# Norm of the output blocks in four parts, feed-forward h rows on GpSimd's queue, and first h rows of the last embedding block ahead of its weights

## The chip, the cores and the metric

The kernel runs on one core of a Trainium2 chip. A core has a matrix engine (TensorE, PE in the profile, with PEld for its weight loads), a vector engine (VectorE, DVE), a scalar engine (ScalarE, ACT), GpSimd (POOL) and a sync engine (SyncE, SP) that here only issues transfers. Each of them works through its own queue of instructions in order. Transfers between the chip's memory (HBM, tensors named `_d` here) and the core's working memory (SBUF) are issued from SP, ACT and POOL. The matrix engine writes its sums into eight accumulator banks (PSUM).

The metric is the device time of one execution in microseconds (us). Before the change it is 2998.36 us, the median of three runs from 2993.83 to 3000.24.

## The reference, cut to what matters

One layer of a hybrid decoder on 2048 prompt tokens and 32 sample tokens, 2080 rows in all, with a model width of 1024, all in float32. Everything up to `mix` (projections, recurrence, attention) is the first part of the kernel and is not touched. What the change touches is the second part:

```python
mix = concat(o_a, o_b)                       # (tokens, 1024)
h = x + mix @ w_o

hn = rmsnorm(h, norm_ffn_g)
u = hn @ w_gate                              # D_FF = 2816
c = conv_b + sum(conv_w[j] * shifted(u, j) for j in range(3))
h = h + (silu(c) * (hn @ w_up)) @ w_down

gate = sigmoid(rmsnorm(h, norm_ple_g) @ w_ple_gate)
h = h + gate * (p_emb @ w_ple_proj)          # PLE_DIM = 256
y = rmsnorm(h, norm_final_g)
```

`rmsnorm(x, g)` is `x * rsqrt(mean(x * x) + 1e-6) * g` along the width of 1024.

## The kernel before

**Tiling.** The second part is the function `trunk`. Activations lie transposed: a tile has 128 features as partitions and tokens along it, so that the width of 1024 makes `NK` = 8 tiles, called rows here (row m of h is `h[m]`, 128 features by a block's tokens). The tokens make three blocks of 696, 696 and 688 (`TRUNK`, L38). Every float32 product is made of three matmuls of rounded halves (`mm3`, L144): high by high, high by low and low by high. So weights and activations are split into a high and a low half, by a cast on ACT and a subtraction on DVE (`split_to`, L183 to L186; `halves`, L1085).

**Stages.** Nine blocks run one after the other (L1559 to L1565): output blocks 0, 1, 2 (`out_block`, the product with w_o), feed-forward blocks 0, 1, 2 (`ffn_block`), embedding blocks 0, 1, 2 (`embed_block`). Each has a generator (`out_prep`, `ffn_prep`, `embed_prep`) that loads and splits its input rows; the block before runs it ahead in steps (`ahead`, `s.to`). Between the stages the rows go through HBM: `h_d` (h after w_o), `hn_d` (its norm times the gain), `h2_d` (h after the feed-forward part). The profile leaves a trailing digit out of a name, so both `h_d` and `h2_d` stand in it as `h_d`; the line tells them apart (L1431 loads h_d, L1314 stores and L1447 and L1483 load h2_d).

**Output block.** It multiplies by w_o row by row, adds x, stores the row to h_d (L1128) and sums squares. The norm comes in two delayed steps in the queue `late` (L1091, L1172): `cols` makes the reciprocal root of each token's mean square; `norm` (L1159) spreads it over the partitions by matmuls against the identity and then, for each of the eight rows, multiplies by it and by the gain on DVE (L1162) and stores the row to hn_d (L1163). `flush(n)` runs up to n entries of `late`. Blocks 0 and 1 are flushed in the next output block (L1115 the first entry, L1140 after m == 2 the rest); block 2 is flushed in feed-forward block 0, at f == 2, one entry after product 5 and one after product 4 of the gate (L1349). Block 2's rows lie in the pool of eight `held` tiles (L1122), and a held tile is free again when its last user, for norms the store to hn_d, is done.

**Feed-forward block.** It goes over 22 tiles of the width of 2816 in pairs (f = 0, 2, ... 20). A pair's product with w_gate, and then with w_up, is a 2 by 2 block product in seven instead of eight products (`strassen`, L1243), made in the order `USE` = 1, 5, 6, 7, 4, 2, 3. After products 1, 6 and 7 the accumulator is copied out on ACT (`copied`, L1254, tile `s`); DVE adds combine banks (L1265, L1269, L1271). `after_gate(n)` and `after_up(n)` are called after product n and put in between what else is due: pieces of the down product (`down`) and `flush`. In block 0 the weight combinations are made on GpSimd (`factors`, L168) and stored; in blocks 1 and 2 they are loaded.

**Down product.** Two pairs at a time (the eleventh alone) are multiplied with w_down, again in seven products in the order `DOWN_USE` = 1, 6, 7, 4, 5, 3, 2 (`downs`, L1286). Their weights are fetched from `wd_d` on GpSimd's queue (L1296, 512 KB each, into six tiles), two products ahead. DVE adds each sum into a row of h (L1312). `ADD` (L1284) says into which half: products 1, 6, 3 and 2 go to rows 0 to 3, products 7, 4 and 5 to rows 4 to 7. The h rows are loaded from h_d at the end of f == 2, into held tiles (L1428 to L1431), and after the last group each finished row is stored to h2_d (L1313, L1314). The last group of a block is left to the start of the next block (L1325) or, in block 2, done at its end (L1435).

**Embedding block.** `embed_prep` loads the h2 rows, scales and splits them, and then loads and splits the two rows of pT. `embed_block` makes the first two (block 2: three) rows of the product with w_ple_gate for all k at once (`dense_first`, L1475), runs one entry of `late`, and asks for the first two h2 rows again (`more`, L1485 and L1486) for the addition at L1502. Each later `embed` asks for one more. The tiles come from `wide`, 44 of 128 by 696, which most of the trunk shares; raw weights from a pool of seven, split ones from a pool of six.

**What sets the order.** The program is written in the order above, but a planner sets each engine's queue from the program's order (earlier is more urgent), the dependencies, the free tiles and its own estimate of times (`schedule_with_timeline_sim`, L1687). A transfer written late can be put early if its tile is free. Once the queues are set, each engine waits at its next instruction.

## Time and profile before

| | before |
|---|---|
| median of 3 runs | 2998.36 us (2993.83 to 3000.24) |
| profiled execution | 2996.88 us |
| its span, first to last instruction | 2995.1 us |
| mean granted clock of the matrix engine | 0.987 |
| PE busy from 1850 to 2000 us | 146.88 of 150 us |
| PE busy from 2000 to 2200 us | 200.00 of 200 us |
| PE busy from 2900 to 2950 us | 46.27 of 50 us |
| h rows loaded from h_d (L1431) | 24, first and last issue at 1436.9 and 2315.4 us |
| rows stored to h2_d (L1314) | 24, from 1837.2 to 2740.4 us |
| rows loaded again from h2_d (L1483) | 24, from 2746.4 to 2939.0 us |
| down weights from wd_d (L1296) | 231 |

The profile's times are in us from the start of the span. A page gives the busy time of each engine; the 40 slices give the busy share in tenths; the view of waits sums up who waited for whom ("PE mm L146 <- ACT s L1254" is PE, about to run a matmul of line 146 into tile mm, held up by the instruction of line 1254 on ACT); the timeline lists instructions with start, length and, in brackets, the idle time before them and what ended it. SPq stands for SP's queue of transfers. "x3" behind a row means three merged ones, whose length runs from the first to the last.

The time up to about 1215 us belongs to the first part. Output blocks run to about 1390 us, feed-forward block 0 to about 1830, block 1 to about 2270, block 2 to about 2740, and the embedding blocks to the end.

### The profile page before, as it was taken

How to read it: one execution, taken by the hardware profiler on the slowest of the kernel's cores; microseconds unless marked ns; L12 is line 12 of the kernel's file. 1: busy time of each engine (PE TensorE's matmuls, PEld its weight loads, DVE VectorE, ACT ScalarE, POOL GpSimd, SP SyncE). 2: the span in 40 equal slices, each digit the busy share in tenths (PEclk: the TensorE clock that was granted, in tenths of full speed). 3: DMA queues.
4: the chain of work that ended last, by engine and by line, in shares of the span. 5: the costliest groups of instructions: out<-in, count | busy, mean ns of one | idle time of the engine just before them, and what ended most of it. 6: DMA issues, size and time to landing. Idle time of an engine off the chain costs nothing.

```text
span 2995.1 us, 52434 instructions
## 1 busy us (share of the span) xinstructions
PE 2899.1 (97%) x18895; PEld 2700.5 (90%) x18895; DVE 2163.4 (72%) x4717; ACT 1318.4 (44%) x2856; POOL 674.0 (23%) x792
## 2 busy tenths in 40 slices
PE   8999999999989898999999999999999999999998
PEld 8987789887777677999999999999999999999998
DVE  6656758657386467569987888766679777677777
ACT  5333423222276576335444444544444544444443
POOL 1443222212143563103443431000001000000000
PEclk9999999999999999999999999999999999999998
DMA  5898634324349996766766668777779777778773
GB/s 179 297 355 305 206 105 120 99 80 124 123 114 279 249 234 177 258 233 210 243 203 204 203 200 293 236 242 243 252 242 308 251 237 243 245 261 295 267 268 132
DMA packets 342036, 659.88 MB, mean 220 GB/s; under 512 B 62928, under 2 KB 134736, under 8 KB 339984
## 3 DMA queue, kind: packets, MB, share of 16 engines
q1 hardware_dynamic: 304928, 468.42, 49.0%
q0 software_dynamic: 33264, 121.13, 12.8%
q10 hardware_dynamic: 3584, 66.98, 6.2%
q8 instruction: 149, 2.44, 0.3%
q14 instruction: 111, 0.91, 0.1%
HBM read 509.46 MB, written 213.92 MB: 242 GB/s over the span
## 4 chain that ended last, share of the span: by engine, by line
PE 59%; issue 17%; DMA 10%; DVE 9%; POOL 2%; ACT 2%; SPq 1%; POOLq 0%; DVEq 0%; ACTq 0%
PE mm L146 13%; PE mm L148 13%; PE mm L147 13%; PE mm L348 2%; PE mm L349 2%; PE mm L350 2%; POOL w L1296 1%; DMA cf<-coef_d 1%; PE acc L839 1%; PE PT L827 1%; PE S L814 1%; DMA xr<-in_xT_dram 1%; PE lv L485 1%; DVE w L185 1%; DMA draw<-in_w_down_dram 1%
## 5 line engine op out<-in xcount | busy, mean ns | idle before, releaser
L147 PE MATMUL mm<-w 128*128 128x348 f32 (+3 forms) x3636 | 1166.1, 321 | 1.3 <-DVE w L1456 0.8
L146 PE MATMUL mm<-w 128*128 128x348 f32 (+3 forms) x3508 | 1108.7, 323 | 18.7 <-ACT s L1254 6.2
L148 PE MATMUL mm<-w 128*128 128x348 f32 (+3 forms) x3508 | 1117.3, 321 | 2.0 <-DVE w L185 2.0
L147 PEld LDWEIGHTS mm<-w 128*128 128x128 f32 x3636 | 684.1, 188 | 4.1 <-DVE w L1088 2.0
L146 PEld LDWEIGHTS mm<-w 128*128 128x128 f32 x3508 | 656.2, 188 | 26.6 <-ACT s L1254 8.7
L148 PEld LDWEIGHTS mm<-w 128*128 128x128 f32 x3508 | 659.0, 188 | 3.3 <-DVE w L185 2.6
L185 DVE TENSOR_TENSOR w<-raw,w 128x512 fp32r<-128x512 f32 x586 | 421.1, 723 | 176.2 <-ACT w L184 168.6
L184 ACT CAST w<-raw 128x512 fp32r<-128x512 f32 x586 | 360.9, 621 | 413.1 <-PE mm L148 288.8
L1296 POOL DMA_DIRECT2D w<-wd_d x231 | 124.3, 538 | 899.2 <-PE mm L148 793.4
L1312 DVE TENSOR_TENSOR h<-h,mm 128x348 f32<-128x348 f32 (+1 forms) x504 | 247.7, 507 | 44.8 <-PE mm L148 43.5
L820 ACT ACTIVATE P<-P,st 128x256 f32<-128x256 f32 (+3 forms) x256 | 134.0, 526 | 60.0 <-DVE st L819 56.4
L1254 ACT COPY s<-mm 128x348 f32<-128x348 f32 (+1 forms) x198 | 88.0, 445 | 152.2 <-PE mm L148 151.9
L819 DVE CUSTOM_DVE_ANT_0 P<-S,mask 128x256 f32<-128x256 f32 (+3 forms) x256 | 104.4, 448 | 62.0 <-PE S L815 40.2
L348 PE MATMUL mm<-wh,xh 128*128 128x512 f32 x352 | 140.8, 403 | 0.1
L349 PE MATMUL mm<-wl,xh 128*128 128x512 f32 x352 | 140.7, 401 | 0.2 <-DVE wl L271 0.2
L350 PE MATMUL mm<-wh,xl 128*128 128x512 f32 x352 | 140.3, 399 | 0.0
L146 PE MATMUL mm<-xh,wh 128*128 128x384 f32 (+2 forms) x384 | 124.6, 329 | 8.0 <-ACT xh L246 5.2
L148 PE MATMUL mm<-xh,wl 128*128 128x384 f32 (+2 forms) x384 | 124.4, 328 | 4.2 <-DVE wl L271 4.2
L147 PE MATMUL mm<-xl,wh 128*128 128x384 f32 (+2 forms) x384 | 125.0, 328 | 1.2 <-DVE xl L247 1.2
L185 DVE TENSOR_TENSOR dw<-draw,dw 128x512 fp32r<-128x512 f32 x77 | 75.3, 981 | 54.0 <-ACT dw L184 53.6
L152 POOL TENSOR_SCALAR wh<-wraw 128x512 fp32r<-128x512 f32 x96 | 75.3, 798 | 133.3 <-PE mm L147 41.6
L814 PE MATMUL S<-kH,qS 128*128 128x256 f32 (+3 forms) x256 | 98.6, 400 | 6.7 <-DVE st L819 4.2
(346 smaller groups left out, 5053.2 us busy)
## 6 DMA issues: line engine op xcount, KB each, us to landing
w<-wd_d POOLq DMA_DIRECT2D x231, 512.0 KB, 5.5
wd_d<-dw SPq DMA_DIRECT2D x77, 512.0 KB
out_sk_dram<-in_cache_k_dram ACTq DMA_DIRECT2D x56, 584.0 KB
out_sv_dram<-in_cache_v_dram ACTq DMA_DIRECT2D x56, 584.0 KB
raw<-in_w_gate_dram SPq DMA_DIRECT2D x110, 256.0 KB
raw<-in_w_up_dram SPq DMA_DIRECT2D x110, 256.0 KB
wraw<-in_w_in_dram SPq DMA_DIRECT2D x104, 256.0 KB
raw<-w_gate_d SPq DMA_DIRECT2D x88, 256.0 KB
```

The source lines that it names most:

```text
L146: PE.matmul(ps, lhsT=wh, rhs=xh, start=first, stop=False, skip_group_check=read)
L147: PE.matmul(ps, lhsT=wh, rhs=xl, start=False, stop=False, skip_group_check=read)
L148: PE.matmul(ps, lhsT=wl, rhs=xh, start=False, stop=last, skip_group_check=read)
L184: A.copy(w[:, 0], raw)
L185: V.tensor_sub(w[:, 1], raw, f32(w[:, 0]))
L348: PE.matmul(ps, lhsT=xh[k][:, js], rhs=wh, start=k == 0, stop=False)
L349: PE.matmul(ps, lhsT=xh[k][:, js], rhs=wl, start=False, stop=False)
L350: PE.matmul(ps, lhsT=xl[k][:, js], rhs=wh, start=False, stop=k == NK - 1)
L814: PE.matmul(s[:, w * i:w * i + w], lhsT=bl.q(hh), rhs=bl.k(kH, hh), start=True, stop=False)
L820: A.activation(pe, pe, AF.Exp, bias=mn, scale=-1.0, accum_out=st[:, bl.r, hh, 0:1])
L1296: G.dma_start(t, wd_d[p][n - 1])
L1312: V.tensor_add(o, o, acc[m][:, :H])
```

## The change

It does four things:

- `norm` of an output block is cut into four entries of `late`, each for two rows; the first also does the spreading over the partitions. The default of `flush` goes from 2 to 5. In feed-forward block 0 at f == 2 the entries are run after products 5 and 4 as before, and after 2 and 3 of the gate and product 1 of up.
- The stores to h2_d are issued on GpSimd's queue instead of SP's, in all three blocks.
- The loads of h_d are issued on GpSimd's queue in blocks 1 and 2; in block 0 they stay on SP's.
- In embedding block 2 the first two `more()` are written ahead of the weights of `dense_first`; in blocks 0 and 1 they stay behind it.

```diff
-        def flush(n=2):
+        def flush(n=5):
...
-            def norm():
-                steps.pop()()
-                for m in range(NK):
+            def norm(m0):
+                if m0 == 0:
+                    steps.pop()()
+                for m in (m0, m0 + 1):
                     V.scalar_tensor_tensor(h[m], h[m], gains[:, 1, m:m + 1], rbs[0], op0=ALU.mult, op1=ALU.mult)
                     SP.dma_start(hn_d[:, m, t0:t0 + T], h[m])
...
-            late.extend((cols, norm))
+            late.append(cols)
+            late.extend([lambda m0=m0: norm(m0) for m0 in range(0, NK, 2)])
...
                     if ps[-1] == PAIRS - 1 and n in (5, 2):
-                        SP.dma_start(h2_d[:, m + 4 * i, t0:t0 + T], h[m + 4 * i])
+                        G.dma_start(h2_d[:, m + 4 * i, t0:t0 + T], h[m + 4 * i])
...
-                    if f == 2 and n in (5, 4):
+                    if f == 2 and n in (5, 4, 2, 3):
                         flush(1)
...
                 def after_up(n):
 
+                    if f == 2 and n == 1:
+                        flush(1)
...
                     for m in range(NK):
-                        SP.dma_start(h[m], h_d[:, m, t0:t0 + T])
+                        (G if b else SP).dma_start(h[m], h_d[:, m, t0:t0 + T])
...
             rb, steps = rstd(s.ssq, T)
-            first = dense_first([weight(I["w_ple_gate"][m]) for m in range(n1)], chunks, xh, xl, mid=steps)
-            flush(1)
             h = []
...
-            more()
-            more()
+            if b == 2:
+                more()
+                more()
+            first = dense_first([weight(I["w_ple_gate"][m]) for m in range(n1)], chunks, xh, xl, mid=steps)
+            flush(1)
+            if b < 2:
+                more()
+                more()
             wpp = [weight(I["w_ple_proj"][128 * k:128 * k + 128], dw) for k in range(2)]
```

## The prediction

> **What bounds the kernel now.** I read the page first, for its engines and its 40 slices.

> ```profile
> span 2995.1 us, 52434 instructions
> PE 2899.1 (97%) x18895; PEld 2700.5 (90%) x18895; DVE 2163.4 (72%) x4717; ACT 1318.4 (44%) x2856; POOL 674.0 (23%) x792
> PE   8999999999989898999999999999999999999998
> ```

> The matmul engine is busy for 97% of the span, and in the slices from 1200 us on, where the edited blocks run, at 90% or more. The edit takes no matmul away. All that it can give back is idle time of PE in that part, so the second view is PE's waits from 1200 us to the end (total, times, longest).

> ```profile
> PE mm L146 <- ACT s L1254: 6.2, 7, 2.6
> PE mm L133 <- DVE rs_y L109: 2.9, 2, 2.4
> PE mm L118 <- DVE w L1069: 2.8, 2, 2.1
> PE mm L146 <- DVE w L1500: 2.2, 1, 2.2
> PE mm L146 <- DVE h L1312: 2.1, 7, 0.4
> PE mm L148 <- DVE w L185: 2.0, 2, 1.3
> PE mm L146 <- DVE u L1269: 2.0, 1, 2.0
> PE mm L146 <- DVE w L1495: 1.5, 1, 1.5
> PE mm L146 <- DMA w<-wd_d: 1.1, 1, 1.1
> PE mm L147 <- DVE w L1456: 0.8, 1, 0.8
> ```

> The ten rows add up to 23.6 us, which is 0.8% of the span and the ceiling for any gain here. The L133 and L118 rows lie mostly in the last norm, which is not edited. The third view is the timeline around the single long waits; three of them stand beside an edited step, and each edit is costed there.

> **Edit 1, the norm in parts.** Blocks 0 and 1 leave their norm to the next output block. There, after m == 2, flush() runs whatever is left; its count goes from 2 to 5 so that it still takes all four parts at once, and nothing moves. Only output block 2 changes: its norm runs inside the feed-forward block 0, at f == 2, as eight multiplications and eight stores in one go. Vector engine and PE there:

> ```profile
> 1431.66 8.93 DVE L1162 SCALAR_TENSOR_TENSOR h<-h,c_gains,w 128x688 f32<-128x688 f32 x8 [0.44 <-ACT w L142]
> 1440.52 0.51 DVE L1269 TENSOR_TENSOR u<-mm,s 128x348 f32<-128x348 f32 x1
> 1441.17 0.40 PE L146 MATMUL mm<-w 128*128 128x348 f32 x1 [1.97 <-DVE u L1269]
> ```

> The eight hold DVE for 8.93 us; the add that empties an accumulator bank (L1269) queues behind all of them, and PE loses 1.97 us. In four parts, spread over products 4, 2 and 3 of the gate and product 1 of up, such an add waits for at most one part, 8.93 / 4 = 2.2 us instead of up to 8.9. No work is removed: 8.93 us of DVE stay, and DVE is full behind it.

> ```profile
> 1440.00:1450.00 10.00, 8.83 (x55) 8.86 (x56) 10.00 (x14) 6.18 (x11) 2.88 (x1) 1.00 0.99 365
> 1450.00:1460.00 10.00, 10.00 (x65) 10.00 (x64) 9.96 (x21) 5.43 (x11) 3.29 (x3) 1.00 0.74 275
> ```

> (Columns: the stretch, then busy time of PE, weight loads, DVE, ACT and POOL, granted clock, DMA share, GB/s.) From 1450 on PE is busy for all 10 of 10 us although DVE is still full, so the rest of the DVE queue had slack. I take the whole 1.97 us as the gain. The other end is a loss of the same size, 2.0, if a later part now stands ahead of another urgent add. The eight stores on SP's queue spread with the parts, so the h tiles they free come later by a few us, and with them the eight h loads on SP. That is covered: rows 4 to 7 are first used by the third down product, after the first two have added into rows 0 to 3. I count this at nothing; without that cover it would be one wait like the one of edit 2.

> **Edit 2, the h transfers on GpSimd's queue.** SP's order in the trace is not the program's: the planner put the h loads of f == 2 (L1431) and the h2 stores (L1314) of the block before between the weight loads of the new block (L1011). SP's queue at the border of blocks 0 and 1, then its waits there, then who paid:

> ```profile
> 1819.49 0.33 SPq L1011 DMA_DIRECT2D raw<-w_up_d  x1
> 1837.19 1.60 SPq L1314 DMA_DIRECT2D h_d<-h  x3
> 1841.77 0.32 SPq L1431 DMA_DIRECT2D h<-h_d  x1
> 1842.19 0.50 SPq L1314 DMA_DIRECT2D h_d<-h  x1
> 1843.40 7.50 SPq L1431 DMA_DIRECT2D h<-h_d  x3
> 1850.95 0.55 SPq L1011 DMA_DIRECT2D raw<-in_w_gate_dram  x1
> ```
> ```profile
> SPq L1314 <- DVE h L1312: 18.2, 3, 17.4
> SPq L1431 <- DMA h_d<-h: 10.4, 5, 4.9
> ```
> ```profile
> 1861.92 0.62 ACT L184 CAST w<-raw 128x512 fp32r<-128x512 f32 x1 [3.57 <-DMA raw<-w_gate_d]
> 1864.80 0.42 PE L146 MATMUL mm<-w 128*128 128x348 f32 x1 [2.59 <-ACT s L1254]
> ```

> SP stands 17.4 us at the first h2 store, which waits for DVE's last adds, and 4.9 us at an h load that waits for a store to land. No weight is asked for from 1819.49 to 1850.95. A weight half then comes 3.57 us late to ACT, the copy L1254 queues behind its cast, and PE loses 2.59 us. With both kinds on POOL's queue the weight loads wait for their own buffers alone. If they come more than 3.57 us earlier, ACT's wait and PE's 2.59 go; the 4.9 us alone are enough. Next late is then ACT's ordinary work: the other six PE waits on L1254 share 6.2 - 2.6 = 3.6 us. At the border of blocks 1 and 2 the same edit is made, but the ten rows hold no second long wait for it, so I count nothing there.

> What it costs: 24 stores and 16 loads more on POOL (block 0's eight loads stay on SP). POOL's rows are the down-weight fetches, first their durations (ns min/median/max) and landing, then those after the border:

> ```profile
> L1296 POOL DMA_DIRECT2D w<-wd_d x231: 530/530/748, 1206.7 to 2722.8; - x116
> ```
> ```profile
> DMA to landing us min/median/max: 3.7/5.5/13.3
> ```
> ```profile
> 1878.88 0.53 POOL L1296 DMA_DIRECT2D w<-wd_d  x1 [32.44 <-PE mm L148]
> 1906.27 0.53 POOL L1296 DMA_DIRECT2D w<-wd_d  x1 [26.86 <-PE mm L148]
> ```

> 40 x 0.53 = 21 us of POOL, in gaps of 27 and 32 us at this border: nothing on the path. Queued behind a store that waits for DVE are only fetches for products tens of us away. The first use of the loaded rows is the add of the next block:

> ```profile
> 1903.19 0.94 DVE L1312 TENSOR_TENSOR h<-h,mm 128x348 f32<-128x348 f32 x2 [0.31 <-PE mm L148]
> ```

> A load issued before 1878.88 and landing in at most 13.3 us is there by 1892. So edit 2 gains 2.59 us; its ends are 0 and, if half of those 3.6 us went too, 4.4.

> [...]

> **Edit 3, the last block's first h rows.** SP, DVE and PE at the start of embedding block 2:

> ```profile
> 2900.83 0.38 SPq L1462 DMA_DIRECT2D w<-in_pT_dram  x1
> 2907.52 1.53 SPq L1011 DMA_DIRECT2D raw<-in_w_ple_gate_dram  x3
> 2909.15 4.17 SPq L1483 DMA_DIRECT2D w<-h_d  x6
> ```
> ```profile
> 2915.68 0.61 DVE L1502 TENSOR_TENSOR w<-w 128x432 f32<-128x432 f32 x1 [3.63 <-DMA w<-h_d]
> 2916.99 0.47 PE L146 MATMUL mm<-w 128*128 128x432 f32 x1 [1.49 <-DVE w L1495]
> 2920.69 0.47 PE L146 MATMUL mm<-w 128*128 128x432 f32 x1 [2.25 <-DVE w L1500]
> ```

> SP stands from 2901.2 to 2907.5 at weights without a free buffer; the h rows (L1483) queue behind them, the first lands 6.5 us after 2909.15, and DVE idles 3.63 us. Behind it stand the reads that free two banks, so PE loses 1.49 + 2.25 = 3.74. Two rows ahead of the weights go out near 2901 and land near 2907.5, before the add could start (2915.68 - 3.63 = 2912.05). Everything on DVE then moves up by 3.63: the first bank is free before PE asks, the second 3.63 earlier, which leaves 3.74 - 3.63 = 0.1. The gain is 3.6 us. The two loads pass six weight halves, which go out 2 x 0.38 us later (the pT load's duration); SP's stand of 6.3 us covers that. The other end is 0, if the two tiles are not free before 2909. The third row is still loaded at 2909 and wanted three adds later; 6.5 us cover it.

> **Sum.** 1.97 + 2.59 + 3.6 = 8.2 us. The profiled execution took 2996.88 us: its span of 2995.1 and 1.8 around it; it lies 1.5 below the median of 2998.36. So 2988.7 for it, and **2990.2** against the median, 0.27% faster. The three runs before lie between 2993.83 and 3000.24, so 0.2% (6.0 us) is about what a measurement can tell from no change: under 2992.4 counts as faster, over 3004.4 as slower.

> **The rivals.**
> *Only issue time is saved.* The weights at the first border are late because the transfers share the wires, not the queue. For it stands the border's own row, with a DMA share of 1.02:

> ```profile
> 1840.00:1850.00 10.00, 9.74 (x62) 9.46 (x61) 10.00 (x17) 7.01 (x13) 1.06 (x2) 1.00 1.02 340
> ```

> Against it: SP issued nothing for 17.4 us. Edit 2 gives nothing, 2998.36 - 5.6 = 2992.8. [...] Chance 0.15.
> *The h rows' tiles are late.* Edit 3 changes the order on SP only; 2998.36 - 4.6 = 2993.8. For it: all six loads go out in a row at 2909, as if tiles came free together. Against it: the pT load before them found a tile at 2900.83. Chance 0.14.
> *The change does not do what it says.* The planner orders anew and puts the parts back to back, or a wait as long as those removed opens elsewhere. Time 2998.4, chance 0.15.
> *Slower: rows behind a fetch.* On POOL the last h loads are placed behind a fetch that waits for PE, such as that of 1906.27. The row lands at 1906.27 + 0.53 + 5.5 = 1912.3 and DVE's first add stands 9.1 us; edit 3's rows show PE losing as much as DVE stands. At both borders this is 18.2 - 8.2 = 10 us more, 3008.4. It decides when a load is issued after about 1903.19 - 5.5 = 1897.7; on SP the loads went out from 1841.77 on. Chance 0.08.

> **How the numbers follow.** The forecast has 0.48. Of it some 0.41 lies under 2992.4, of the first two rivals 0.09: faster 0.50. The last rival is slower, 0.08. The rest, 0.42, is no change. The range must reach the third rival to hold 8 in 10: up to 3000, its time and the spread of the runs. Down it goes to 2986: the forecast with edit 2 at its upper end (2990.2 - 1.8 = 2988.4) and 2 us of spread.

> **What would show it.** Right: no PE wait over 1 us on L1269 near 1440; SP without a stand at the borders, and ACT's 3.57 us on w_gate_d gone; no DVE wait of L1502 on h_d; PE's waits from 1200 us on down from 23.6 to some 15.5. Wrong: DVE adds (L1312) that wait for h_d, POOL standing at stores with a late fetch behind, or a new PE wait on L184 or L185 between 1440 and 1470.

## The result and the profile after

| | before | after |
|---|---|---|
| median of 20 runs each | 2994.95 us (2987.18 to 3002.88) | 2988.86 us (2982.62 to 2995.76) |
| profiled execution | 2996.88 us | 2983.43 us |
| its span | 2995.1 us | 2981.7 us |
| mean granted clock | 0.987 | 0.987 |

The ratio is 0.9981, 95% interval 0.9973 to 0.9989: 6.1 us or 0.19% faster. The gain is real, since the interval leaves out 1, and it lies just on the inner side of the 0.2% that the prediction called no change. The forecast had 2990.2 us and a gain of 8.2. The time came out 1.3 us below it only because 20 runs of the kernel before have a median 3.4 us below that of the first three; as a gain the forecast was 2.1 us too high.

The engines and, behind them, the waits of PE from 1200 us to the end, both of the kernel after:

```profile
PE 2897.5 (97%) x18895; PEld 2701.9 (91%) x18895; DVE 2161.8 (73%) x4717; ACT 1318.5 (44%) x2856; POOL 696.1 (23%) x832
```
```profile
PE mm L146 <- ACT s L1256: 5.0, 8, 1.3
PE mm L133 <- DVE rs_y L109: 2.9, 2, 2.4
PE mm L118 <- DVE w L1069: 2.8, 2, 2.1
PE mm L146 <- DVE h L1314: 2.0, 7, 0.4
PE mm L146 <- DVE u L1271: 2.0, 1, 2.0
PE mm L148 <- DVE w L185: 1.7, 1, 1.7
PE mm L146 <- DMA w<-wd_d: 1.1, 1, 1.1
PE mm L146 <- DVE w L1508: 0.9, 1, 0.9
PE mm L147 <- DVE w L1460: 0.7, 1, 0.7
```

POOL has the 40 more instructions (832 for 792) and 22 us more work. PE's waits add up to 19.1 us instead of 23.6: 4.5 less, where the forecast had 8.1 (23.6 to 15.5). The lines of the code have moved by two to eight: L1256 is the copy that was L1254, L1271 the add that was L1269, L1508 and L1510 the multiplication and the add that were L1500 and L1502. The longest copy wait is down from 2.6 to 1.3 and the two waits at the embedding are down to one of 0.9, but the wait of 2.0 on L1271, the whole of edit 1, stands as it was.

**The norm.** The eight multiplications and the add behind them, on DVE, and PE's matmul that waits for it:

```profile
1425.38 8.94 DVE L1163 SCALAR_TENSOR_TENSOR h<-h,c_gains,w 128x688 f32<-128x688 f32 x8 [0.44 <-ACT w L142]
1434.24 0.51 DVE L1271 TENSOR_TENSOR u<-mm,s 128x348 f32<-128x348 f32 x1
```
```profile
1434.89 0.40 PE L146 MATMUL mm<-w 128*128 128x348 f32 x1 [1.97 <-DVE u L1271]
```

Four entries of `late` or one: the queue has the eight in one piece, with the same 1.97 us behind them. Compared instruction by instruction, PE, DVE and ACT run the same instructions in the same order before and after; only those of POOL and SP differ, from the first h2 store on.

**The border of feed-forward blocks 0 and 1.** SP's queue, then SP's waits from 1805 to 1860, then the moved transfers on POOL:

```profile
1813.21 0.33 SPq L1011 DMA_DIRECT2D raw<-w_up_d  x1
1838.93 0.33 SPq L1011 DMA_DIRECT2D raw<-in_w_gate_dram  x1
1839.96 6.60 SPq L1011 DMA_DIRECT2D raw<-w_gate_d  x3
```
```profile
SPq L1011 <- DVE w L185: 49.3, 12, 25.3
```
```profile
1835.28 0.55 POOL L1435 DMA_DIRECT2D h<-h_d  x1 [0.92 <-DMA h_d<-h]
...
1849.85 0.54 POOL L1435 DMA_DIRECT2D h<-h_d  x1 [4.12 <-DMA h_d<-h]
...
1853.44 0.54 POOL L1435 DMA_DIRECT2D h<-h_d  x1 [0.66 <-DMA h_d<-h]
1870.58 0.54 POOL L1298 DMA_DIRECT2D w<-wd_d  x1 [16.61 <-PE mm L148]
```

This execution runs 6.3 us ahead here, so stretches have to be compared, not times. Before, the next weight was asked for 1850.95 - 1819.49 = 31.5 us after the last w_up_d; now 1838.93 - 1813.21 = 25.7, which is 5.7 us sooner. It is no sooner than that because those loads stand 25.3 us for their own raw buffers, which DVE's subtraction (L185) frees. POOL stands 4.1 us at a load where SP stood 4.9, and nothing urgent is behind it. The last load goes out at 1853.44, ahead of the fetch at 1870.58 that waits for PE.

**The start of embedding block 2.** SP, DVE and PE:

```profile
2892.97 0.90 SPq L1485 DMA_DIRECT2D w<-h_d  x2
2898.83 1.57 SPq L1011 DMA_DIRECT2D raw<-in_w_ple_gate_dram  x3
2900.49 1.80 SPq L1485 DMA_DIRECT2D w<-h_d  x4
```
```profile
2903.79 0.61 DVE L1510 TENSOR_TENSOR w<-w 128x432 f32<-128x432 f32 x1
```
```profile
2909.27 0.47 PE L146 MATMUL mm<-w 128*128 128x432 f32 x1 [0.90 <-DVE w L1508]
```

Two rows go out ahead of the weights, and the add L1510 carries no bracket: it no longer waits for a row. PE has one wait of 0.90 in place of 1.49 + 2.25.

**Where the 13.4 us between the two spans lie.** For this I take when PE starts its matmul of the same number (both kernels have 18,895 in the same order):

| stretch of PE's matmuls | before, us | after, us | difference |
|---|---|---|---|
| start of the span to no. 8000 | 1233.1 | 1227.3 | 5.8 |
| no. 8000 to 9400 (norm of block 2) | 224.50 | 224.03 | 0.5 |
| no. 11,800 to 12,100 (border of blocks 0 and 1) | 50.63 | 48.58 | 2.05 |
| no. 18,000 to the last (embedding blocks 1 and 2) | 150.12 | 144.95 | 5.2 |

They hold all of it. The 5.8 us lie ahead of everything that the change touches, where all queues are the same: one execution differs from another by so much. That is why the medians are 6.1 apart and the two profiles 13.4. The last row is more than the idle time that went, 3.74 - 0.90 = 2.84 us, and the clock says why. Windows of the kernel before around its two waits, then of the kernel after around its one (columns as in the prediction; their counts of matmuls are not compared, since small and large ones are mixed):

```profile
2914.90:2921.50 6.60, 2.87 (x14) 2.06 (x13) 5.68 (x21) 2.44 (x5) 0.00 (x0) 1.00 0.42 167
2921.50:2924.90 3.40, 3.40 (x17) 3.31 (x15) 0.68 (x3) 0.87 (x2) 0.00 (x0) 0.50 0.00 0
2924.90:2931.50 6.60, 6.60 (x36) 6.31 (x35) 6.03 (x8) 1.65 (x4) 0.00 (x0) 1.00 0.65 255
```
```profile
2908.20:2911.60 3.40, 2.50 (x17) 2.28 (x17) 2.52 (x9) 0.94 (x2) 0.00 (x0) 1.00 0.00 0
```

Behind the two waits PE was granted half its clock for 3.4 us. From the start of the matmul behind the last of the waits to that of the 21st after it PE needs 4.84 us before and 3.22 us after: the half clock costs 1.62 us, about half of its 3.4. So 2.84 + 1.62 = 4.5 of the 5.2. With the short wait the clock stays at 1.00.

### The profile page after: what moved, and what is told of

Its sections match the earlier page's. It is cut to its first block, busy times and chain, and to the rows that moved or that the text cites. A ratio compares the mean times of both kernels' runs of the same rounds, so it can differ in the third digit from the quotient of the medians.

```text
span 2981.7 us, 52460 instructions
## 1 busy us (share of the span) xinstructions
PE 2897.5 (97%) x18895; PEld 2701.9 (91%) x18895; DVE 2161.8 (73%) x4717; ACT 1318.5 (44%) x2856; POOL 696.1 (23%) x832
## 3 DMA queue, kind: packets, MB, share of 16 engines
q8 instruction: 149, 2.44, 0.3%
## 4 chain that ended last, share of the span: by engine, by line
PE 76%; DVE 9%; DMA 8%; issue 3%; ACT 2%; POOL 2%; SPq 1%; DVEq 0%; POOLq 0%; ACTq 0%
PE mm L146 19%; PE mm L147 19%; PE mm L148 19%; PE mm L348 2%; PE mm L349 2%; PE mm L350 2%; DMA cf<-coef_d 1%; PE acc L839 1%; DMA draw<-in_w_down_dram 1%; PE S L814 1%; PE PT L827 1%; PE lv L485 1%; DVE h L1314 1%; DMA wd_d<-dw 1%; PE S L815 1%
## 5 line engine op out<-in xcount | busy, mean ns | idle before, releaser
L147 PE MATMUL mm<-w 128*128 128x348 f32 (+3 forms) x3636 | 1166.3, 321 | 0.8 <-DVE w L1460 0.7
L146 PE MATMUL mm<-w 128*128 128x348 f32 (+3 forms) x3508 | 1109.1, 323 | 13.9 <-ACT s L1256 5.0
L148 PE MATMUL mm<-w 128*128 128x348 f32 (+3 forms) x3508 | 1117.3, 321 | 1.7 <-DVE w L185 1.7
L147 PEld LDWEIGHTS mm<-w 128*128 128x128 f32 x3636 | 684.3, 188 | 3.5 <-DVE w L1088 1.6
L146 PEld LDWEIGHTS mm<-w 128*128 128x128 f32 x3508 | 656.8, 188 | 21.5 <-ACT s L1256 7.3
L148 PEld LDWEIGHTS mm<-w 128*128 128x128 f32 x3508 | 659.1, 188 | 2.8 <-DVE w L185 2.0
L185 DVE TENSOR_TENSOR w<-raw,w 128x512 fp32r<-128x512 f32 x586 | 420.3, 722 | 173.4 <-ACT w L184 166.3
L184 ACT CAST w<-raw 128x512 fp32r<-128x512 f32 x586 | 361.2, 621 | 409.6 <-PE mm L148 298.3
L1314 DVE TENSOR_TENSOR h<-h,mm 128x348 f32<-128x348 f32 (+1 forms) x504 | 247.9, 507 | 44.9 <-PE mm L148 43.3
L1256 ACT COPY s<-mm 128x348 f32<-128x348 f32 (+1 forms) x198 | 87.9, 444 | 155.6 <-PE mm L148 155.2
L146 PE MATMUL mm<-xh,wh 128*128 128x384 f32 (+2 forms) x384 | 125.3, 331 | 7.4 <-ACT xh L246 5.0
L148 PE MATMUL mm<-xh,wl 128*128 128x384 f32 (+2 forms) x384 | 125.2, 330 | 3.0 <-DVE wl L271 2.9
L147 PE MATMUL mm<-xl,wh 128*128 128x384 f32 (+2 forms) x384 | 125.5, 329 | 1.1 <-DVE xl L247 1.1
L185 DVE TENSOR_TENSOR dw<-draw,dw 128x512 fp32r<-128x512 f32 x77 | 73.0, 954 | 51.7 <-ACT dw L184 49.7
L271 DVE TENSOR_TENSOR wl<-wraw,wh 128x512 fp32r<-128x512 f32 x104 | 85.3, 841 | 27.4 <-POOL wh L152 22.8
```

Of the source, the lines that this page charges most:

```text
L146: PE.matmul(ps, lhsT=wh, rhs=xh, start=first, stop=False, skip_group_check=read)
L147: PE.matmul(ps, lhsT=wh, rhs=xl, start=False, stop=False, skip_group_check=read)
L148: PE.matmul(ps, lhsT=wl, rhs=xh, start=False, stop=last, skip_group_check=read)
L184: A.copy(w[:, 0], raw)
L185: V.tensor_sub(w[:, 1], raw, f32(w[:, 0]))
L1314: V.tensor_add(o, o, acc[m][:, :H])
```

## The experiments

The theory after the result: edits 2 and 3 each remove the stall that they stand beside, and edit 1 is no change of the program. The rivals: the norm edit does something that the trace does not show; the two others gain only together, or by something else than the queue named; DVE is so full around the norm that no order of it could help. Six kernels were timed over 10 to 12 executions each, against 34 or 21 of the kernel before on the same chip; the four others have one profiled execution each. Single executions of one kernel lie up to 19 us apart (2982.82 to 3001.93 of the norm really spread), so for these the waits and the stretches of PE decide, not the time. A wait or a stretch is always that of one execution, the profiled one.

**Edit 1 alone.** The kernel before with the norm in four entries, nothing else:

```diff
-            late.extend((cols, norm))
+            late.append(cols)
+            late.extend([lambda m0=m0: norm(m0) for m0 in range(0, NK, 2)])
...
-                    if f == 2 and n in (5, 4):
+                    if f == 2 and n in (5, 4, 2, 3):
```

> The norm in four parts alone. Theory A (the planner puts the eight multiplications back to back anyway, as in the profile after): eight L1162 rows in one piece of 8.9 us, the PE wait of 1.97 us on the add behind them is still there, and the time is that of before within 0.2%. Rival (the parts do spread, and their gain is taken back by something else in the changed kernel): the wait is gone here, 2.0 us less.

Measured: 2996.45 us against 2997.24, ratio 0.9998 (0.9987 to 1.001). DVE around the norm:

```profile
1436.67 8.94 DVE L1163 SCALAR_TENSOR_TENSOR h<-h,c_gains,w 128x688 f32<-128x688 f32 x8 [0.38 <-ACT w L142]
1445.53 0.51 DVE L1271 TENSOR_TENSOR u<-mm,s 128x348 f32<-128x348 f32 x1
```

All five engines run the same instructions in the same order as in the kernel before, but for one MEMSET of 0.06 us that starts ahead of its neighbour on DVE. So the edit is no change of the program. A reason that fits, not shown by a run: the planner takes the order of the program as urgency among instructions that could run, the eight multiplications could run from the same moment on and the add could not yet, so they go first, however the entries are cut. This pair also shows what the measurement does with the same queues: 0.02% by the ratio, with an interval of a tenth of a per cent to either side.

**Edit 2 alone.** The kernel before with both kinds of transfer on GpSimd's queue:

```diff
-                        SP.dma_start(h2_d[:, m + 4 * i, t0:t0 + T], h[m + 4 * i])
+                        G.dma_start(h2_d[:, m + 4 * i, t0:t0 + T], h[m + 4 * i])
...
-                        SP.dma_start(h[m], h_d[:, m, t0:t0 + T])
+                        (G if b else SP).dma_start(h[m], h_d[:, m, t0:t0 + T])
```

> The h stores and h loads on GpSimd's queue, nothing else. Theory A: PE's wait at the border of feed-forward blocks 0 and 1 falls from 2.59 to 0.54 us, as after, and PE is 2.05 us ahead from there to the embedding blocks; the waits of 1.5 and 2.2 us at the start of embedding block 2 stay, with the half clock behind them. Time 2 us (0.07%) under before, which a timing cannot tell from no change. Rival (only issue time is saved): the 2.59 us stay.

Measured: 2993.59 us against 2997.24, ratio 0.999 (0.9977 to 1.0002). The time alone would not settle it; the waits of PE from 1825 to 1880 us do:

```profile
PE mm L146 <- DVE h L1312: 0.9, 3, 0.4
PE mm L146 <- ACT s L1254: 0.5, 1, 0.5
```

The copy wait is 0.54 instead of 2.59, and the stretch of the border takes 48.57 us, 2.05 less than before. At the embedding start both waits stay, 0.7 and 2.3 us here for 1.49 and 2.25, and the half clock with them.

**Edit 3 alone.** The kernel before with the two `more()` of embedding block 2 ahead of `dense_first`:

```diff
+            if b == 2:
+                more()
+                more()
             first = dense_first([weight(I["w_ple_gate"][m]) for m in range(n1)], chunks, xh, xl, mid=steps)
```

> The first h rows of the last embedding block ahead of its weights, nothing else. Theory A: this is the largest part: the two waits shrink from 3.74 to 0.9 us as after, and the 3.4 us of half clock that follow them in the profile before do not come, together some 5 us (0.17%). Rival (the half clock comes on its own account, whatever the waits): it is still there near 2921 us and the gain is some 3 us.

Measured: 2992.09 us against 2997.24, ratio 0.9986 (0.9975 to 0.9996). PE's waits from 2880 to 2940 us:

```profile
PE mm L146 <- DVE w L1504: 0.9, 1, 0.9
```

The last stretch of PE takes 145.05 us for 150.12, with no half clock. So this edit alone is a gain that the timing can tell from none, and it and edit 2 add up: 0.14% and 0.10% alone, 0.19% together, with an interval of 0.1% to either side of each.

**The stores alone, the loads alone.** Each half of edit 2 by itself, on the kernel before:

```diff
-                        SP.dma_start(h2_d[:, m + 4 * i, t0:t0 + T], h[m + 4 * i])
+                        G.dma_start(h2_d[:, m + 4 * i, t0:t0 + T], h[m + 4 * i])
```

> Of the queue edit the stores to h2_d alone; the loads of h_d stay on SP. Theory A (SP stands at an h load until a store has landed, and that is what makes the weight half late; the 17.4 us stand at the first store cost nothing, since in the changed kernel the weight loads wait for their own buffers just as long): SP still stands some 5 us at the loads and PE's wait at the border of feed-forward blocks 0 and 1 stays near 2 us. Rival (the stores' wait for DVE was the harm): the wait falls to 0.54 us.

```diff
-                        SP.dma_start(h[m], h_d[:, m, t0:t0 + T])
+                        (G if b else SP).dma_start(h[m], h_d[:, m, t0:t0 + T])
```

> Of the queue edit the loads of h_d alone; the stores to h2_d stay on SP. Theory A: PE's wait at that border falls to 0.54 us as with both. Rival (the stores' wait for DVE was the harm): it stays near 2 us.

Measured, one execution each: 2994.94 and 2989.77 us, with 2993.20 for one of the kernel before beside them. SP's longest waits from 1805 to 1865 us, first with the stores alone moved, then with the loads alone moved:

```profile
SPq L1431 <- DMA h_d<-h: 26.1, 5, 21.4
SPq L1011 <- DVE w L185: 21.4, 10, 10.1
```
```profile
SPq L1011 <- DVE w L185: 25.8, 12, 10.1
SPq L1314 <- DVE h L1312: 21.5, 6, 17.4
```

| kernel | next weight behind the last w_up_d | ACT's longest wait for a w_gate_d half | PE's wait on L1254 | stretch of the border |
|---|---|---|---|---|
| before | 31.5 us | 3.57 | 2.59 | 50.63 |
| edit 1 alone (this border as before) | 31.1 | 3.01 | 1.96 | 51.55 |
| edit 3 alone (this border as before) | 30.4 | 2.44 | 1.42 | 49.45 |
| stores alone | 27.0 | 0.65 | 0.54 | 48.58 |
| loads alone | 25.7 | 1.13 | 0.54 | 48.57 |
| both (edit 2 alone) | 25.7 | none | 0.54 | 48.57 |

The first three rows have the same queues here, and their wait is not the same: PE's is ACT's less 1.0 us in each, so about 1.0 us of a late half costs nothing. The 2.59 of the kernel before is the largest of the three; edit 2 takes 0.9 to 2.05 us of idle time, and by the stretch 1.97 at their mean of 50.54 (in the row of edit 1 alone 3.4 us at half clock follow the wait). Either half brings the whole gain. The expectation for the stores alone had given them none, and it falls: SP still stands 21.4 us, now at a load, and yet the weights come 4.5 us sooner, which is more than the 3.57 by which they were late. And with the loads alone moved SP keeps the very 17.4 us stand at the first store on which the prediction had leaned, at no cost at all. Why either half is enough the runs leave open; in the kernel before, stores and loads take turns on SP, and with one kind gone they no longer do.

**The norm really spread.** The kernel after, with parts two to four tied in the queue behind an add of the Strassen product, so that the planner cannot pull them together:

```diff
+        def behind():
+            if late:
+                with tc.issue_after(mark[-1].ins):
+                    flush(1)
...
-            put(1, 1, lambda o, v: V.tensor_add(o, v(pb), v(s3)))
+            put(1, 1, lambda o, v: mark.append(V.tensor_add(o, v(pb), v(s3))))
...
-                    if f == 2 and n in (5, 4, 2, 3):
+                    if f == 2 and n in (5, 4):
                         flush(1)
+                    elif f == 2 and n == 3:
+                        behind()
...
-                    if f == 2 and n == 1:
-                        flush(1)
+                    if f == 2 and n in (4, 3):
+                        behind()
```

> The changed kernel, with parts two, three and four of the norm each tied behind an add of DVE that empties a bank. Theory A (the eight multiplications in a row are what PE waits for): no PE wait over 0.5 us there, 2.0 us less than the changed kernel; against before 0.9974 in place of 0.9981. Rival (DVE is full around it, so that another add or weight half comes late in place of this one): as much idle time of PE between 1420 and 1480 us as after, 2 us or more, at other places.

Measured: 2990.79 us against 2997.24, ratio 0.9982 (0.9966 to 0.9998), no different from the kernel after. DVE, then PE's waits from 1430 to 1460 us:

```profile
1433.93 2.82 DVE L1163 SCALAR_TENSOR_TENSOR h<-h,c_gains,w 128x688 f32<-128x688 f32 x2 [0.37 <-ACT w L142]
1436.68 0.51 DVE L1278 TENSOR_TENSOR u<-mm,s 128x348 f32<-128x348 f32 x1
1437.11 2.38 DVE L1163 SCALAR_TENSOR_TENSOR h<-h,c_gains,w 128x688 f32<-128x688 f32 x2
```
```profile
PE mm L148 <- DVE w L185: 1.3, 2, 0.7
PE mm L146 <- ACT s L1263: 0.5, 1, 0.5
```

Now the add goes after two multiplications and the wait of 1.97 is gone, but 1.85 us of others came up, for weight halves and a copy. Spread as the edit meant it, the norm gains 0.1 us of idle time in this execution.

**The norm cut.** Is it DVE's fill that makes those waits? The kernel after without the multiplications of six of block 2's eight rows, which go on without their norm and gain:

```diff
                 for m in (m0, m0 + 1):
-                    V.scalar_tensor_tensor(h[m], h[m], gains[:, 1, m:m + 1], rbs[0], op0=ALU.mult, op1=ALU.mult)
+                    if b < 2 or m < 2:
+                        V.scalar_tensor_tensor(h[m], h[m], gains[:, 1, m:m + 1], rbs[0], op0=ALU.mult, op1=ALU.mult)
```

> The changed kernel without the multiplication of six of the eight rows in the norm of output block 2 (these rows go on without their norm and gain). Takes 6.7 us of DVE away. Theory B (DVE is full there, so its work and not its order is what PE pays; the run with the parts held moved the waits and kept their sum): the idle time of PE between the first product of feed-forward block 0 and f == 4 falls by 2 us. Rival (PE waits there for other things in turn, casts on ACT and transfers): it falls by less than 1 us, with other waits in place of the 1.97.

Measured, one execution: 2988.58 us. PE's waits from 1430 to 1460 us:

```profile
PE mm L148 <- DVE w L185: 0.8, 1, 0.8
PE mm L146 <- ACT s L1257: 0.5, 1, 0.5
PE mm L146 <- ACT w L1421: 0.2, 1, 0.2
```

With 6.7 us of DVE work gone, 1.5 us of waits remain, and 0.5 of the 1.97 is saved. So the theory that the norm's share of DVE's work makes them falls: at this place the weight halves, combined on GpSimd, cast on ACT and subtracted on DVE, and a copy are next late. No order of the norm tried here gained more than these 0.5 us. The cut is not quite clean, for the planner also orders SP's queue anew from 1344 us on and PE's from 1369.

**The rest of the embedding's wait.** The theory: with edit 3, DVE reaches L1508 late because the small steps of block 1's last norm sit ahead of it. The kernel after with these steps tied behind the add of row 2, and the rest of that flush two rows later:

```diff
-            flush(1)
             if b < 2:
+                flush(1)
                 more()
...
-                V.tensor_add(h[m][:, cs], h[m][:, cs], gt_[:, cs])
+                add = V.tensor_add(h[m][:, cs], h[m][:, cs], gt_[:, cs])
...
-                if m == 2:
+                if b == 2 and m == 2 and late:
+                    with tc.issue_after(add.ins):
+                        flush(1)
+                if m == (2 if b < 2 else 4):
                     flush()
```

> The changed kernel, with the small DVE steps of the last-but-one norm (about 13 of 0.15 us, between the first adds of embedding block 2) tied behind the add of its row 2. Theory A (what is left of that wait, 0.9 us, is DVE's queue with these small steps in it): the 0.9 us fall under 0.4. Rival (it is the chain of matmul, sigmoid and multiplication by itself): they stay within 0.2 of 0.9.

Measured, one execution: 2987.13 us. Between 2880 and 2945 us PE has no wait left, and the last stretch takes 143.89 us for 144.95. To see whether a timing can tell it, this kernel and the kernel after were timed side by side:

> The changed kernel once more, on the chip of the next run. Theory A: 0.9975 to 0.9985 of before. Its profile has waits of 0.5 and 0.9 us in place of 2.6 and 3.7, the 2.0 us at the norm as before, and no half clock near 2910 us.

> The changed kernel with the small norm steps tied behind the add of row 2, timed. Theory A: 1.0 us under the changed kernel (the 0.9 us wait is gone), which is 0.03% and below what the timing tells; against before 0.9975 to 0.9985 as well. Rival (the wait comes back later in the block, since PE has to wait for the held norm): no difference in the trace at the end of the block.

Measured: 2991.41 us for the kernel after and 2989.94 us for the one with the steps held, both against 2996.18: ratios 0.9982 (0.9972 to 0.9992) and 0.9979 (0.997 to 0.9989). Their last stretches take 145.29 and 144.08 us. By the trace the version with held steps is about 1 us better than the kernel after; by the timing it can't be told from it. The kernel after came out with nearly the same ratio as the first time (0.9982 for 0.9981).

## Why the prediction was right or wrong

**Edit 1, 1.97 us: wrong, it gave nothing.** The step that failed was "in four parts, spread over products 4, 2 and 3 of the gate and product 1 of up, such an add waits for at most one part": the parts were never spread. This was the third rival, the planner putting them back to back, applied to one edit. The second step, "the rest of the DVE queue had slack", fails as well: really spread, the norm exchanges 1.97 us of waits for 1.85, and with most of it cut 1.5 remain. That PE was busy for all 10 of 10 us behind the stall did not mean slack on DVE.

**Edit 2, 2.59 us: right in kind, 2.05 in size.** The weights come sooner, ACT's wait of 3.57 goes (0.34 is left in the kernel after), POOL pays nothing that matters. The term was too large because the copy keeps a wait of 0.54, the same in all nine kernels with the edit or half of it; the prediction named the ordinary copy waits as next late and then left them out of the sum. It also took one execution's 2.59 for the kernel's, where two others with the same queues have 1.96 and 1.42. The reading of SP's stand was wrong: most of the 31.5 us without a weight is the wait for raw buffers, 25.3 us once the queue is free. What the queue added was 5.7 us, and of the half's lateness on ACT all but about 1.0 us reached PE. The first rival, that only issue time is saved, falls with it. The slower rival, rows placed behind a fetch, falls by the row of 1853.44: all loads were out 17 us before the next waiting fetch. On the moved issues (busy us, mean ns, then POOL's idle time before them and what ended it):

```profile
L1316 POOL DMA_DIRECT2D h_d<-h x24 | 13.1, 546 | 21.9 <-DVE h L1314 17.5 <-DVE rs_t L107 2.0 <-DMA h<-h_d 1.4
L1435 POOL DMA_DIRECT2D h<-h_d x16 | 8.6, 538 | 18.1 <-DMA h_d<-h 16.5 <-issue 1.5
```

The 40 issues took 13.1 + 8.6 = 21.7 us against an estimate of 21. The stores landed 5.7 us after their issue at the median and the loads 6.0, none after more than 8.4, with DVE busy for 73% of the span.

**Edit 3, 3.6 us: right in kind, about 4.1 in size.** Between the two profiles 2.84 us of idle time went and not 3.6: the step "Everything on DVE then moves up by 3.63" overlooked the small norm steps that were hidden in DVE's wait, and 0.90 stayed where 0.1 was forecast. The 3.74 was also the largest of five: the other kernels without the edit wait 2.6 to 3.2 us here, so at the mean of 3.1 some 2.2 us of idle time went. The clock, for which the sum has no term, gave most of the rest: 1.6 us of the half clock behind the waits. The 23.6 us that the prediction called the ceiling were not one, since they leave this out. Over the kernels, the last stretch is 149.05 us at the mean of the five without the edit and 144.97 at that of the five with it and nothing further. The rival of late tiles falls: both rows went out at 2892.97, right behind the pT load.

**The sum.** 0 + 2.05 + 4.1 = 6.1 us, which is what the medians of 20 runs say (with the 1.97 of the table's mean, 6.0). That it agrees to a tenth is luck, with each term known to some tenths at best. Against the forecast, 1.97 us of edit 1 never came, edit 2 was 0.5 too large and edit 3 was 0.5 too small; the last made the forecast look closer, and that too is luck, for there a lost clock that the sum did not count made up for idle time that stayed. Of the signs named for being right, ACT's wait of 3.57 and DVE's wait on h_d are gone; the wait near 1440 stands, SP still stands at the border for its buffers, and PE's waits are 19.1 us and not 15.5. The measured gain of 0.19% lies on the bound of 0.2% between faster and no change, so these runs can't say which of the two chances, 0.50 and 0.42, was the better.

## What to carry to other kernels

Where a planner orders the queues, a statement moved in the program is a wish: look in the trace at which instructions could run at that moment, and expect no change if the moved ones could run and the urgent one could not. A queue that stands costs only what the instruction behind it could have used (with the loads alone moved, SP's 17.4 us at the first store cost PE nothing): take off the wait that it would then meet on its own, and ask by how much the consumer is really late. When a long wait on the matrix engine is removed, look at the granted clock behind it; here the 1.62 us given back there were more than half as much again as the 2.84 of idle time. The same wait of 2.0 us had a half clock behind it in four of ten kernels here, so look at several executions.

## What the hardware showed beyond what was expected

The half clock is the surprise. At the embedding start, where PE waits twice within 7 us (0.4 to 1.5 us, then 2.3) and works through six matmuls in between, all five kernels without edit 3 had a stretch of 3.4 us at 0.50 right behind, and none of the seven with it. It also came behind a single wait: behind the 2.0 us at the norm, four of the ten kernels that have this wait were slowed, and behind the 1.96 us at the border edit 1 alone was, though the kernel before was not behind its 2.59. These are two windows of the kernel with edit 3 alone, the one with the wait and the one behind it; then the same of the kernel with edit 2 alone; then the two windows of the kernel before that share its wait:

```profile
1439.30:1442.70 3.40, 1.37 (x9) 1.12 (x8) 3.40 (x6) 1.61 (x3) 0.00 (x1) 0.99 0.95 353
1442.70:1446.10 3.40, 3.40 (x14) 3.40 (x13) 3.40 (x4) 1.18 (x2) 2.86 (x1) 0.50 0.92 265
1439.50:1442.90 3.40, 1.53 (x10) 1.56 (x11) 3.40 (x6) 2.54 (x4) 1.00 (x1) 1.00 1.06 330
1442.90:1446.30 3.40, 3.40 (x23) 3.40 (x23) 3.40 (x5) 1.88 (x4) 1.88 (x1) 1.00 0.86 308
1436.67:1440.09 3.42, 2.53 (x16) 2.25 (x15) 3.42 (x4) 1.48 (x3) 0.65 (x1) 1.00 1.00 314
1440.09:1443.50 3.41, 2.33 (x15) 2.36 (x16) 3.41 (x7) 1.95 (x3) 1.80 (x1) 1.00 1.05 391
```

That is what was measured at this one place, and no rule for others: in five kernels one such piece between 2721 and 2738 us was at 0.50 although PE was busy for 0.79 to 0.80 of the one ahead (0.80 in the kernel before, at 2730.3 us, and in the kernel after, at 2721.3). Why stays open.

One execution also differs from another, with the same queues on all engines, by 5.8 us in the first 1230 us (by 10.5 between the furthest two of the twelve) and at one copy near 1420 us (1.3 us of wait in four, 2.3 to 2.4 in seven, five of them with a half clock behind). Where from stays open; against gains of 2 to 4 us it means that single executions decide nothing by their time.
